# A decoder trunk on one core: the low halves of split weights made by another engine, a mean shift moved off TensorE, and 52 weight blocks multiplied in wider instructions

## The chip, the core and the metric

The kernel runs on one core of one Trainium2 chip. The core has a matrix engine (TensorE; PE in the profile, PEld for its weight loads), three engines for elementwise work (VectorE = DVE, ScalarE = ACT, GpSimd = POOL), an engine that mostly issues DMAs (SyncE = SP), and 16 DMA engines. Each engine works through its own queue in order; queues wait for each other by semaphores. The metric is the device time of one execution in microseconds, lower is better; the median of several runs is quoted.

## What is computed

Two decoder layers on one sequence of 256 tokens, model width 2048, everything in float32. Layer 0 mixes by causal pooling, layer 1 by dilated attention; each is followed by a gated feed-forward network with a short causal convolution, and each of the four sub-blocks ends in `h = layer_norm(alpha * h + sub_block(h))` with alpha = 4^(1/4). Cut to what matters here:

```python
def layer_norm(x, g, b):
    mu = jnp.mean(xf, axis=-1, keepdims=True)
    var = jnp.mean(jnp.square(xf - mu), axis=-1, keepdims=True)
    y = (xf - mu) * lax.rsqrt(var + LN_EPS) * g + b
...
def pool_mixer(h, w_in, w_grp, scale, w_out):
    p = h @ w_in                       # 2048 x 2048, four groups of 512 channels
    pooled = trailing means over 2, 4, 8, 16 tokens, minus p
    mixed = per group pooled @ w_grp, * scale
    return mixed @ w_out
...
def conv_ffn(h, w_up, conv_w, conv_b, w_down):
    c = causal width-3 convolution of (h @ w_up) + conv_b
    gate, val = jnp.split(c, 2, axis=-1)
    return (jax.nn.silu(gate) * val) @ w_down      # hidden width 5504
...
for i in range(2):
    mix = pool_mixer(h, ...) if i == 0 else dilated_attention(h, k_shared, v_shared, ...)
    h = layer_norm(ALPHA * h + mix, ln1_g[i], ln1_b[i])
    h = layer_norm(ALPHA * h + conv_ffn(h, ...), ln2_g[i], ln2_b[i])
```

The weights are some 380 MB and are read from HBM once.

## The kernel before

**Precision.** A float32 product is made from float32r products by splitting both factors into a high part (the value rounded to float32r) and a low part (the value minus its high part): high x high, high x low and low x high are summed, low x low is dropped. An activation tile is stored as `[128, 4, 2, 258]`: four blocks of 128 channels, high and low part, 256 tokens and two more columns.

**Units.** The weights are cut into 364 units of mostly 512 x 512 (four row blocks of 128, four column blocks of 128, 1 MB); a few have three row or column blocks. `group` (L153) and `group_tm` (L162) append units; four units in a row (or three or two, in the down-projections) sum up into the same four PSUM banks, and the last of them calls `post`, which empties the banks. `run_units` (L102) does the units in order. For unit i it first calls `ahead(i)` (L87), then issues unit i's matmuls, then the functions that earlier units put off with `later(n, fn)`, then `post`. All of it is written out by hand in program order; each engine's queue has that order.

**Loads and splits.** `do_load` (L60) brings unit i + 5 from HBM by SyncE's queue into one of three raw tiles, so a load waits until the split of the unit three before has let go of its tile. `do_split` (L70) runs three units ahead of TensorE and makes `wh` (high) and `wl` (low), with four tiles each. There are two ways. Two units in three: ScalarE rounds raw to `wh` (L82), VectorE computes `wl = raw - wh` (L83). Every third unit from unit 6 on: ScalarE writes `wl = -raw` rounded (L77), then `wh` (L78), and a DMA issued by GpSimd adds raw to `wl` in memory (L79). Either way the raw tile is free when `wl` is done.

**Matmuls.** `mm_quad` (L126) does a unit with the weights stationary. For each row block k and column block m, mode "ab" issues two matmuls: `wh` on high and low part of the activations side by side (512 columns, L141), and `wl` on the high part (256 columns, L142); high and low products land in the two halves of a bank, and `post` has to add the halves. Modes "a" and "x" issue three matmuls of 256 (258) columns into the same half: L144, L145, L146. In the last unit of a group the column blocks are done one after another, so that their banks can be emptied one after another. `group_tm` uses the activations as the stationary side, with 512 columns of weights (L170 to L172).

**Which units have which mode.** The up-projections from the third pair of groups on, the down-projections of layer 0 apart from the last, and the attention's projections for K and Q from the second group on are "ab". The pooling's input projection (`add_in`, L462), its group products, the second pair of up-projection groups of each layer, and everything that goes through `add_last` (L398) are "a": the pooling's output projection (16 units), the attention's output projection (16) and the last part of layer 0's down-projection (12 units, four of them of three row blocks). The first groups behind a LayerNorm are "x".

**Residual and LayerNorm.** `resid_last(c)` (L242) adds bank m to block m of `H[c]` (L247, L249), the quarter c of the stream, while TensorE is still at the next block. To keep sums of squares small, a per-token shift, found from the first quarter (`shift`, L289: a matmul with ones, L291, a unit after quarter 0), is taken off the whole stream. For quarter 0 VectorE subtracts it (L299). For the others: where the sub-block is the first to be added to H (both mixers), the subtraction is part of the scaling by alpha in `pre` (L311); in the last down-projection of layer 0 it is instead a thirteenth product for each bank, a matmul of one row, minus ones times the shift (L148, with `neg1` from L216). Then follow sums and sums of squares (`fold`, L270), the scaled copies `XP` that the "x" units use (`xp`, L316), and the statistics (`chain`, L326) with normalisation of H by VectorE (`norm`) and the affine step and the split of the activations (`affine`, `lo`) in the units after.

**Pooling.** `pool_post` (L406) copies the banks out by ScalarE (L412) and builds window sums on VectorE (L416 to L423).

Of the kernel before, what the change touches and what calls it, by code (L numbers as in the profile page):

```python
# [10 lines left out]
F32R = mybir.dt.float32r  # L11
I32 = mybir.dt.int32
AF = mybir.ActivationFunctionType
OP = mybir.AluOpType
# [3 lines left out]
T = 256  # L18
P = 128
# [3 lines left out]
ALPHA = 4.0 ** 0.25  # L23
# [9 lines left out]
def trunk(ctx: ExitStack, tc: tile.TileContext, x, pool_w_in, pool_w_grp, pool_scale, pool_w_out,  # L33
          attn_w_q, attn_w_o, shared_w_k, shared_w_v, ffn_w_up, ffn_conv_w, ffn_conv_b, ffn_w_down,
          ln1_g, ln1_b, ln2_g, ln2_b, out):
    nc = tc.nc
    V, A, PE = nc.vector, nc.scalar, nc.tensor
    ctx.enter_context(tc.manual_schedule())

    const = ctx.enter_context(tc.tile_pool(name="const", bufs=1))  # L40
# [13 lines left out]
    raw, wh, wl = {}, {}, {}  # L54
# [15 lines left out]
    def do_split(i):  # L70
        r = raw.pop(i)
        shape = [P, r.shape[1], r.shape[2]]
        wh[i] = wp.tile(shape, F32R, name=f"wh{i}", tag="wh")
        wl[i] = wp.tile(shape, F32R, name=f"wl{i}", tag="wl")
        if i >= 4 and i % 3 == 0:

            A.activation(wl[i], r, AF.Copy, scale=-1.0)  # L77
            A.copy(wh[i], r)  # L78
            nc.gpsimd.dma_start(wl[i], r, accum_op=OP.add)  # L79
            return  # L80
        for j, s in enumerate(pieces(i, r.shape[1])):
            A.copy(wh[i][:, s], r[:, s])  # L82
            V.tensor_tensor(wl[i][:, s], r[:, s], wh[i][:, s].bitcast(F32), OP.subtract)  # L83
            if i == 0 and j == 0:
                x_quad(0, (1,))
# [37 lines left out]

    XW = T + 2

    def mm_quad(xq, ps, first, last, mode, mid, shifted):  # L126
        def go(h, l):
            nk, nb = h.shape[1], h.shape[2] // P
            order = [(k, m) for k in range(nk) for m in range(nb)]
            if last:  # L130
                order = [(k, m) for m in range(nb) for k in range(nk)]
            if first:
                for m in range(nb):
                    ps.append(bank("acc"))
            q = xq()
            n = XW if mode == "x" else T
            for i, (k, m) in enumerate(order):
                c = slice(m * P, (m + 1) * P)
                st, sp = first and k == 0, last and k == nk - 1
                if mode == "ab":  # L140
                    PE.matmul(ps[m], h[:, k, c], q[:, k, :, :T], start=st, stop=False)  # L141
                    PE.matmul(ps[m][:, :T], l[:, k, c], q[:, k, 0, :T], start=False, stop=sp)  # L142
                else:
                    PE.matmul(ps[m][:, :n], h[:, k, c], q[:, k, 0, :n], start=st, stop=False)  # L144
                    PE.matmul(ps[m][:, :n], h[:, k, c], q[:, k, 1, :n], start=False, stop=False)  # L145
                    PE.matmul(ps[m][:, :n], l[:, k, c], q[:, k, 0, :n], start=False, stop=sp and not shifted)  # L146
                    if sp and shifted:
                        PE.matmul(ps[m][:, :n], neg1[0:1, :], ST["cs"][0:1, :], start=False, stop=True)  # L148
                if mid is not None and i == 7:
                    mid()  # L150
        return go

    def group(w, r0s, c0, ncol, xqs, post, mode="ab", mids=(), shifted=False):  # L153
        ps = []
        for j, (r0, nr) in enumerate(r0s):
            last = j == len(r0s) - 1
            units.append((w[r0:r0 + nr, c0:c0 + ncol],
                          mm_quad(xqs[j], ps, j == 0, last, mode, mids[j] if j < len(mids) else None, shifted),
                          (lambda: post(ps)) if last else None))


# [46 lines left out]
    rows4 = [(512 * j, 512) for j in range(4)]  # L208

    pools = {}  # L210
    H, XC, XP, ST = {}, {}, {}, {}
# [1 line left out]
    ident = const.tile([P, P], F32, name="ident")  # L213
    ones = const.tile([P, 1], F32, name="ones")
    one1 = const.tile([P, P], F32, name="one1")
    neg1 = const.tile([1, P], F32R, name="neg1")  # L216
    ones4 = const.tile([P, P], F32R, name="ones4")
    epst = const.tile([P, 1], F32, name="epst")
    inv = const.tile([P, 1, 16], F32, name="inv")
# [3 lines left out]
    xsrcs = [lambda j=j: XC[j] for j in range(4)]  # L223
# [18 lines left out]
    def resid_last(c, first, lay, which, after):  # L242
        def post(ps):
            for m in range(4):
                y = H[c][:, m, :]
                if first and c == 0:
                    V.scalar_tensor_tensor(y, y, ALPHA, ps[m][:, :T], op0=OP.mult, op1=OP.add)  # L247
                else:
                    V.tensor_tensor(y, y, ps[m][:, :T], OP.add)  # L249
                if c == 3 and m % 2 == 1:  # L250
                    square(3, m - 1)
            if c == 0:
                s = fold(H[0], None, "S0", F32R)
                later(1, lambda: shift(s, first, lay, which))
            elif c < 3:
                n = 3 if c == 1 and not first else 1
                later(n, lambda: stats(c))
                later(n + 1, lambda: xp(c, lay, which))
            else:
                folds(3)  # L260
                xp(3, lay, which)
                later(2, lambda: chain(ps[0], lay, which, after))
        return post
# [25 lines left out]
    def shift(s, first, lay, which):  # L289
        ps = bank("shift")  # L290
        PE.matmul(ps[:, :T], ones4, s, start=True, stop=True)  # L291
        cs = lnp.tile([P, T], F32R, name="cs", tag="cs")
        A.copy(cs, ps[:, :T])
        ST["cs"] = cs
        cb = cs.bitcast(F32).unsqueeze(1).to_broadcast([P, 4, T])
        ST["S"] = ST["Q"] = None

        def one():
            V.tensor_tensor(H[0], H[0], cb, OP.subtract)  # L299
            if first:  # L300
                pre(1)
            stats(0)

        def two():
            xp(0, lay, which)
            if first:
                pre(2)
                pre(3)

        def pre(q):  # L310
            V.scalar_tensor_tensor(H[q], H[q], ALPHA, cb, op0=OP.mult, op1=OP.subtract)  # L311

        later(1, one)
        later(2, two)
# [82 lines left out]

    def add_last(w, rows, srcs, first, lay, which, after=None):  # L398
        for c in range(4):
            group(w, rows, 512 * c, 512, srcs, resid_last(c, first, lay, which, after), mode="a", shifted=c > 0 and not first)  # L400


    PADW = 16
    pooled_q, mixed_q = {}, {}

    def pool_post(g):  # L406
        def post(ps):
            pp = pools["pool"]
            w = 2 << g
            p = pools["pb"][g % 2]  # L410
            for m in range(4):
                A.copy(p[:, m, PADW:], ps[m][:, :T])  # L412
            cur, lo, sh = p, 0, 1
            while sh < w:
                nxt = pp.tile([P, 4, PADW + T], F32, name="sw", tag="sw", bufs=2)
# [3 lines left out]
            n = w - 1  # L419
# [4 lines left out]
                                   op0=OP.mult, op1=OP.subtract)  # L424
# [35 lines left out]
            before.setdefault(min(q + 1, 3), []).append(lambda s=s, pv2=pv2: A.copy(H[q][:, s, :], pv2))  # L460

    def add_in(g, mids=()):  # L462
        group(pool_w_in[0], rows4, 512 * g, 512, xsrcs, pool_post(g), mode="a", mids=mids)

    def add_grp(g):
        group(pool_w_grp[0, g], [(0, 512)], 0, 512, [lambda: pooled_q[g]], grp_post(g), mode="a")
# [189 lines left out]
    scale = 1.0 / math.sqrt(P)  # L656
# [98 lines left out]
    with tc.tile_pool(name="start", bufs=1) as stp:  # L755
# [18 lines left out]
                for i in range(WARM):  # L774
                    PE.matmul(warm[:, :P], one1, one1, start=True, stop=True)
        V.memset(ones, 1.0 / D)
        A.activation(neg1, one1[0:1, :], AF.Copy, scale=-1.0)
        A.activation(ones4, one1, AF.Copy, scale=4.0 / D)
        V.memset(epst, EPS)
        for c in range(16):  # L780
# [108 lines left out]
```

## Time and profile before

| | |
|---|---|
| median of 3 runs | 2100.22 us |
| lowest and highest | 2100.1, 2101.11 us |
| span of the profiled execution, first to last instruction | 2098.8 us |
| HBM read, per span | 380 MB, 182 GB/s |
| DMA engines: share of the loads' queue / of GpSimd's queue | 52.7% / 29.0% |

The profile gives the span of the execution, 2098.8 us, and no other time for it; the device time of the runs contains a little more than from the first to the last instruction. Times are us unless marked ns. A row of groups shows line, engine, operation, output and inputs, shape, count, then busy time and mean duration in ns, then the engine's idle time before these instructions and what ended it. A matmul's own duration is its passage through a pipeline; what a matmul costs in a stream is the distance from its start to the next start. In rows by window the counts of instructions in brackets include those that began before the window; the last three numbers are the granted TensorE clock (1.00 is full speed), the mean busy share of the DMA engines, and GB/s.

### The profile page before, as it was taken

What the parts mean: (1) busy time and instruction counts of PE and PEld (TensorE: products, weight loads), DVE (VectorE), ACT (ScalarE), POOL (GpSimd) and SP (SyncE); (2) the same over time, 40 slices, a digit from 0 to 9 for tenths busy, and PEclk for the clock granted to TensorE, in tenths of its full rate; (3) what the DMA queues carried; (4) which work ended last, traced back from release to release, by engine and by line L of the source; (5) the groups of instructions that cost most, each with busy time, mean ns of one, the idle gap of its engine ahead of it and who ended that gap; (6) DMA issues with size and microseconds to landing.
All of it is one profiled execution on the core that took longest, in us unless ns stands there. A gap on an engine that the chain in (4) does not pass through costs nothing.

```text
span 2098.8 us, 30899 instructions
## 1 busy us (share of the span) xinstructions
PE 2075.0 (99%) x12959; PEld 1863.9 (89%) x12959; DVE 1137.6 (54%) x1586; ACT 1235.0 (59%) x1266; POOL 112.9 (5%) x158
## 2 busy tenths in 40 slices
PE   8999999999999999999999999999999999999997
PEld 8999998888888888899888889999888888888885
DVE  5546575645644655556734555565535553554555
ACT  6555776556645646657755555586646654655663
POOL 2000000000000000000000000000000000000000
PEclk9999999999999999999999999999999999999999
DMA  8888778988888888787887778878888879888885
GB/s 249 272 242 254 221 216 270 276 250 247 240 248 260 250 235 260 221 263 202 232 243 233 221 226 234 238 205 247 241 263 259 260 231 265 246 241 253 233 243 183
DMA packets 212588, 507.59 MB, mean 242 GB/s; under 512 B 8943, under 2 KB 17797, under 8 KB 197985
## 3 DMA queue, kind: packets, MB, share of 16 engines
q1 hardware_dynamic: 194240, 381.71, 52.7%
q0 software_dynamic: 18208, 123.92, 29.0%
q8 instruction: 101, 1.65, 0.3%
q14 instruction: 39, 0.31, 0.0%
HBM read 380.01 MB, written 2.10 MB: 182 GB/s over the span
## 4 chain that ended last, share of the span: by engine, by line
PE 90%; DMA 6%; ACT 1%; issue 1%; DVE 1%; SPq 0%; POOL 0%; DVEq 0%; POOLq 0%; ACTq 0%
PE acc L141 34%; PE acc L142 17%; PE acc L144 8%; PE acc L146 8%; PE acc L145 8%; PE t L170 4%; PE t L171 4%; PE t L172 4%; DMA wl<-raw 4%; DMA raw<-in_ffn_w_down_dram 1%; DMA crow<-in_ffn_conv_w_dram 1%; DMA raw<-in_ffn_w_up_dram 0%; PE s L699 0%; PE o L739 0%; DMA xin<-in_x_dram 0%
## 5 line engine op out<-in xcount | busy, mean ns | idle before, releaser
L141 PE MATMUL acc<-xc,wh 128*128 128x512 f32 x2624 | 924.1, 396 | 0.0
L83 DVE TENSOR_TENSOR wl<-raw,wh 128x2048 fp32r<-128x2048 f32 (+2 forms) x256 | 551.9, 2160 | 522.8 <-ACT wh L82 514.3
L142 PE MATMUL acc<-xc,wl 128*128 128x256 f32 x2624 | 736.2, 281 | 0.0
L82 ACT CAST wh<-raw 128x2048 fp32r<-128x2048 f32 (+2 forms) x256 | 460.1, 1803 | 270.3 <-PE acc L141 128.7
L141 PEld LDWEIGHTS acc<-xc,wh 128*128 128x128 f32 x2624 | 495.0, 189 | 116.6
L142 PEld LDWEIGHTS acc<-xc,wl 128*128 128x128 f32 x2624 | 494.8, 189 | 0.2
L77 ACT ACTIVATE wl<-raw 128x2048 fp32r<-128x2048 f32 (+1 forms) x120 | 226.2, 1885 | 266.4 <-PE acc L142 109.1
L78 ACT CAST wh<-raw 128x2048 fp32r<-128x2048 f32 (+1 forms) x120 | 223.0, 1858 | 0.0
L79 POOL DMA_DIRECT2D wl<-raw x120 | 101.5, 846 | 1933.6 <-ACT wl L77 1484.1
L141 PE MATMUL acc<-g,wh 128*128 128x512 f32 x512 | 179.9, 396 | 0.0
L524 DVE SCALAR_TENSOR_TENSOR c<-u,cv,c 128x256 f32<-128x256 f32 x344 | 144.8, 481 | 41.3 <-ACT c L520 40.4
L146 PE MATMUL acc<-xc,wl 128*128 128x256 f32 x512 | 145.8, 285 | 6.9 <-DMA wl<-raw 6.6
L144 PE MATMUL acc<-xc,wh 128*128 128x256 f32 x512 | 145.4, 284 | 0.9 <-ACT wh L82 0.9
L145 PE MATMUL acc<-xc,wh 128*128 128x256 f32 x512 | 145.0, 283 | 0.0
L142 PE MATMUL acc<-g,wl 128*128 128x256 f32 x512 | 143.6, 280 | 0.0
L171 PE MATMUL t<-wl,g 128*128 128x512 f32 x344 | 135.6, 394 | 1.9 <-DMA wl<-raw 1.9
L170 PE MATMUL t<-wh,g 128*128 128x512 f32 x344 | 136.1, 396 | 0.0
L172 PE MATMUL t<-wh,g 128*128 128x512 f32 x344 | 135.4, 394 | 0.0
L141 PEld LDWEIGHTS acc<-g,wh 128*128 128x128 f32 x512 | 96.6, 189 | 22.8
L145 PE MATMUL acc<-xp,wh 128*128 128x258 f32 x384 | 109.2, 284 | 0.0
L144 PE MATMUL acc<-xp,wh 128*128 128x258 f32 x384 | 109.1, 284 | 0.0
L146 PE MATMUL acc<-xp,wl 128*128 128x258 f32 x384 | 107.9, 281 | 0.0
(195 smaller groups left out, 3055.4 us busy)
## 6 DMA issues: line engine op xcount, KB each, us to landing
raw<-in_ffn_w_up_dram SPq DMA_DIRECT2D x160, 1024.0 KB, 5.6
wl<-raw POOLq DMA_DIRECT2D x111, 1024.0 KB, 7.7
raw<-in_ffn_w_down_dram SPq DMA_DIRECT2D x80, 1024.0 KB, 6.7
raw<-in_pool_w_out_dram SPq DMA_DIRECT2D x16, 1024.0 KB, 6.4
raw<-in_shared_w_k_dram SPq DMA_DIRECT2D x16, 1024.0 KB, 5.3
raw<-in_attn_w_q_dram SPq DMA_DIRECT2D x16, 1024.0 KB, 5.8
raw<-in_shared_w_v_dram SPq DMA_DIRECT2D x16, 1024.0 KB, 5.9
raw<-in_attn_w_o_dram SPq DMA_DIRECT2D x16, 1024.0 KB, 6.0
```

The costliest lines, as they stand in the source:

```text
L77: A.activation(wl[i], r, AF.Copy, scale=-1.0)
L78: A.copy(wh[i], r)
L82: A.copy(wh[i][:, s], r[:, s])
L83: V.tensor_tensor(wl[i][:, s], r[:, s], wh[i][:, s].bitcast(F32), OP.subtract)
L141: PE.matmul(ps[m], h[:, k, c], q[:, k, :, :T], start=st, stop=False)
L142: PE.matmul(ps[m][:, :T], l[:, k, c], q[:, k, 0, :T], start=False, stop=sp)
L144: PE.matmul(ps[m][:, :n], h[:, k, c], q[:, k, 0, :n], start=st, stop=False)
L145: PE.matmul(ps[m][:, :n], h[:, k, c], q[:, k, 1, :n], start=False, stop=False)
L146: PE.matmul(ps[m][:, :n], l[:, k, c], q[:, k, 0, :n], start=False, stop=sp and not shifted)
L170: PE.matmul(ps[t], xh, h[:, k, :], start=j == 0 and k == 0, stop=False)
L171: PE.matmul(ps[t], xh, l[:, k, :], start=False, stop=False)
L172: PE.matmul(ps[t], xl, h[:, k, :], start=False, stop=j == len(r0s) - 1 and k == nk - 1)
```

## The change

Three edits.

1. Every unit is split the first way: `wh` by ScalarE, `wl` by VectorE. The branch with the negated copy and the adding DMA goes.
2. The one-row products go, with `neg1` and the parameter `shifted`. In the last down-projection of layer 0, `pre` now subtracts the shift from quarters 1 to 3 of H on VectorE; `pre(1)` is called in `one`, `pre(2)` and `pre(3)` in `two`, as it is for the mixers.
3. All of `add_last` (44 units) and the pooling's input projection for groups 0 and 1 (8 units) become mode "ab". `resid_last` adds the second half of each bank by a second VectorE addition, `pool_post` likewise for those two groups.

```diff
@@ do_split
-        if i >= 4 and i % 3 == 0:
-
-            A.activation(wl[i], r, AF.Copy, scale=-1.0)
-            A.copy(wh[i], r)
-            nc.gpsimd.dma_start(wl[i], r, accum_op=OP.add)
-            return
         for j, s in enumerate(pieces(i, r.shape[1])):
             A.copy(wh[i][:, s], r[:, s])
             V.tensor_tensor(wl[i][:, s], r[:, s], wh[i][:, s].bitcast(F32), OP.subtract)
@@ mm_quad
-                    PE.matmul(ps[m][:, :n], l[:, k, c], q[:, k, 0, :n], start=False, stop=sp and not shifted)
-                    if sp and shifted:
-                        PE.matmul(ps[m][:, :n], neg1[0:1, :], ST["cs"][0:1, :], start=False, stop=True)
+                    PE.matmul(ps[m][:, :n], l[:, k, c], q[:, k, 0, :n], start=False, stop=sp)
@@ resid_last
                 else:
                     V.tensor_tensor(y, y, ps[m][:, :T], OP.add)
+                V.tensor_tensor(y, y, ps[m][:, T:], OP.add)
@@ shift
         def one():
             V.tensor_tensor(H[0], H[0], cb, OP.subtract)
-            if first:
-                pre(1)
+            pre(1)
             stats(0)
 
         def two():
             xp(0, lay, which)
+            pre(2)
+            pre(3)
+
+        def pre(q):
             if first:
-                pre(2)
-                pre(3)
-
-        def pre(q):
-            V.scalar_tensor_tensor(H[q], H[q], ALPHA, cb, op0=OP.mult, op1=OP.subtract)
+                V.scalar_tensor_tensor(H[q], H[q], ALPHA, cb, op0=OP.mult, op1=OP.subtract)
+            else:
+                V.tensor_tensor(H[q], H[q], cb, OP.subtract)
@@ add_last
-            group(w, rows, 512 * c, 512, srcs, resid_last(c, first, lay, which, after), mode="a", shifted=c > 0 and not first)
+            group(w, rows, 512 * c, 512, srcs, resid_last(c, first, lay, which, after))
@@ pool_post
                 A.copy(p[:, m, PADW:], ps[m][:, :T])
+                if g < 2:
+                    V.tensor_tensor(p[:, m, PADW:], p[:, m, PADW:], ps[m][:, T:], OP.add)
@@ add_in
-        group(pool_w_in[0], rows4, 512 * g, 512, xsrcs, pool_post(g), mode="a", mids=mids)
+        group(pool_w_in[0], rows4, 512 * g, 512, xsrcs, pool_post(g), mode="ab" if g < 2 else "a", mids=mids)
@@ start
-        A.activation(neg1, one1[0:1, :], AF.Copy, scale=-1.0)
```

(The default mode of `group` is "ab".)

More of the change, by code (lines that the diff above doesn't have):

```diff
@@ L124, in trunk, with mm_quad @@
     XW = T + 2
-    def mm_quad(xq, ps, first, last, mode, mid, shifted):
+    def mm_quad(xq, ps, first, last, mode, mid):
         def go(h, l):
@@ L151, in mm_quad, with group @@
         return go
-    def group(w, r0s, c0, ncol, xqs, post, mode="ab", mids=(), shifted=False):
+    def group(w, r0s, c0, ncol, xqs, post, mode="ab", mids=()):
         ps = []
@@ L157, in group @@
             units.append((w[r0:r0 + nr, c0:c0 + ncol],
-                          mm_quad(xqs[j], ps, j == 0, last, mode, mids[j] if j < len(mids) else None, shifted),
+                          mm_quad(xqs[j], ps, j == 0, last, mode, mids[j] if j < len(mids) else None),
                           (lambda: post(ps)) if last else None))
@@ L215, in trunk @@
     one1 = const.tile([P, P], F32, name="one1")
-    neg1 = const.tile([1, P], F32R, name="neg1")
     ones4 = const.tile([P, P], F32R, name="ones4")
@@ L293, in shift @@
         A.copy(cs, ps[:, :T])
-        ST["cs"] = cs
         cb = cs.bitcast(F32).unsqueeze(1).to_broadcast([P, 4, T])
```

## The prediction

> **What bounds the kernel now.** First the page: what is busy, and what the chain that ended last consists of.
>
> ```profile
> span 2098.8 us, 30899 instructions
> PE 2075.0 (99%) x12959; PEld 1863.9 (89%) x12959; DVE 1137.6 (54%) x1586; ACT 1235.0 (59%) x1266; POOL 112.9 (5%) x158
> PE 90%; DMA 6%; ACT 1%; issue 1%; DVE 1%; SPq 0%; POOL 0%; DVEq 0%; POOLq 0%; ACTq 0%
> ```
>
> TensorE is busy for 99% of the span, and nine tenths of the chain that ended last are matmuls. So only two kinds of thing can shorten this kernel: fewer or cheaper steps of TensorE, and fewer waits of TensorE. VectorE and ScalarE have room on average. Next the table of waits, for TensorE and its weight loads alone (total us, how often, longest).
>
> ```profile
> PEld acc L146 <- DMA wl<-raw: 8.3, 5, 5.2
> PE acc L146 <- DMA wl<-raw: 7.1, 3, 5.0
> PEld t L171 <- DMA wl<-raw: 2.3, 1, 2.3
> PE t L171 <- DMA wl<-raw: 1.9, 1, 1.9
> ```
>
> Every wait that matters is for one thing: a low part `wl` that an adding DMA had still to deliver. There are six (five at L146, one at L171), 10.6 us in the weight-load rows. A low part made by VectorE was waited for once:
>
> ```profile
> PE acc L146 <- DVE wl L83: 0.2, 1, 0.2
> ```
>
> The longest wait comes early, in unit 6. The timeline of TensorE and two windows around it (the clock is the entry after the engines):
>
> ```profile
> 46.36 0.28 PE L145 MATMUL acc<-xc,wh 128*128 128x256 f32 x1
> 51.66 0.58 PE L146 MATMUL acc<-xc,wl 128*128 128x256 f32 x1 [5.02 <-DMA wl<-raw]
> 52.04 0.41 PE L144 MATMUL acc<-xc,wh 128*128 128x256 f32 x1
> 52.25 0.41 PE L145 MATMUL acc<-xc,wh 128*128 128x256 f32 x1
> ```
> ```profile
> 46.00:59.00 13.00, 7.98 (x51) 7.78 (x50) 5.92 (x5) 6.01 (x9) 0.00 (x0) 0.74 0.74 224
> 50.00:55.00 5.00, 3.34 (x15) 3.34 (x16) 1.42 (x1) 1.90 (x1) 0.00 (x0) 0.50 0.45 136
> ```
>
> After the wait the steps are 0.21 us apart (52.04 to 52.25), and the granted clock is 0.50 in that window: the stall is paid for a second time, at half clock.
>
> **The change, part by part.** *Low parts by VectorE.* The adding DMAs go, and with them the six waits. The early one: 13.0 us passed for some 49 steps (51 records, of which two began before the window). At 0.119 us a step, derived below, they need 5.8, so this stall costs about 7.1 with its half clock. The other five: 10.6 less 5.2 leaves 5.4; a weight load starts its wait a little ahead of its matmul (5.2 against 5.0 above), so I take 0.1 off each, and put 0.1 back for the slower restart behind it. Together 7.1 + 5.4 = **12.5 us**, if VectorE is in time everywhere. What it takes on, from the groups by shape:
>
> ```profile
> L83 DVE TENSOR_TENSOR wl<-raw,wh 128x2048 fp32r<-128x2048 f32 x225 | 515.4, 2292 | 496.8 <-ACT wh L82 496.1
> L77 ACT ACTIVATE wl<-raw 128x2048 fp32r<-128x2048 f32 x111 | 212.8, 1917 | 242.6 <-PE acc L142 102.0 <-DMA raw<-in_ffn_w_down_dram 47.8 <-PE acc L146 25.1
> L249 DVE TENSOR_TENSOR h<-h,acc 128x256 f32<-128x256 f32 x40 | 15.0, 417 | 14.2 <-PE acc L146 13.2 <-PE acc L148 1.0
> L311 DVE SCALAR_TENSOR_TENSOR h<-h,cs 128x1024 f32<-128x1024 f32 x6 | 7.1, 1220 | 0.0
> ```
>
> 111 whole units at 2.292 us are 254 us, and nine units of three blocks at three quarters of that are 16: VectorE goes from 1138 us to about 1408. ScalarE loses L77: 213 us, and nine small ones at three quarters, some 13; it falls from 1235 to about 1009. Each unit takes TensorE 5.6 to 5.7 us and VectorE 2.3 for its low part, so on average this hides. It must also hide where VectorE is fullest. Those are the stages behind a LayerNorm, where normalising, the convolution and the low parts of the activations share its queue. There a new subtraction delays all that stands behind it in order: the low part of the next unit, and the activations' low parts. The fullest one, in layer 1, by window, then by the rows of VectorE and of the matmul that needs the result:
>
> ```profile
> 1380.00:1410.00 30.00, 30.00 (x253) 30.00 (x252) 23.70 (x31) 28.09 (x36) 1.69 (x2) 1.00 0.68 202
> ```
> ```profile
> 1398.97 1.23 DVE L538 TENSOR_TENSOR c<-u,c 128x1024 f32<-128x1024 f32 x1 [1.55 <-ACT u L537]
> 1400.77 2.29 DVE L83 TENSOR_TENSOR wl<-raw,wh 128x2048 fp32r<-128x2048 f32 x1 [0.57 <-ACT wh L82]
> 1406.24 0.28 PE L146 MATMUL acc<-xc,wl 128*128 128x256 f32 x1
> ```
>
> Two moved units fall into these 30 us: VectorE would have 28.3 of 30, ScalarE 24.3. Bound there is ScalarE today, VectorE afterwards. The walk: the low part of unit 241 ends at 1403.06 and is needed at 1406.24, 3.2 us of slack, the least of any unit behind the first few. In front of it goes the subtraction of unit 240, +2.29; away go VectorE's two waits for ScalarE, 1.55 and 0.57, since ScalarE is 1.9 us earlier by the L77 that it no longer does. Net +0.2: slack stays at about 3.0. I therefore cost this part at nothing, with that slack as the cover; without it, each microsecond of VectorE beyond 3 is a microsecond of TensorE.
>
> The early unit 6 needs its own walk: its raw tile and VectorE before it.
>
> ```profile
> 37.64 1.92 ACT L77 ACTIVATE wl<-raw 128x2048 fp32r<-128x2048 f32 x1 [2.36 <-DMA raw<-in_pool_w_in_dram]
> 40.98 1.16 DVE L423 SCALAR_TENSOR_TENSOR po<-sw,pb 128x964 f32<-128x964 f32 x1
> ```
>
> The raw tile is there at 37.6, so `wh` (now first in ScalarE's queue) is done at 39.6. VectorE is busy with the pooling until 42.1, then subtracts until 44.4. The low part is needed at 46.5, one step after 46.36: 2.1 us to spare.
>
> Loads: a raw slot comes free when its split is done, and the SyncE queue waits for that.
>
> ```profile
> SPq L68 <- DMA wl<-raw: 1342.2, 119, 16.3
> wl<-raw POOLq DMA_DIRECT2D x111, 1024.0 KB, 7.7
> ```
>
> Today a moved unit holds its raw tile for two ScalarE passes and a DMA of 7.7 us (median), 11.5 us in all. Afterwards it is 1.9 + 2.3 = 4.2 us and the time in VectorE's queue. So loads start earlier, the DMA engines lose the second pass over those tiles, and I expect no new wait for a load.
>
> *Shift products.* Twelve one-row matmuls at L148 go. What one costs, from the starts around it:
>
> ```profile
> 921.48 0.28 PE L145 MATMUL acc<-g,wh 128*128 128x256 f32 x1
> 921.61 0.28 PE L146 MATMUL acc<-g,wl 128*128 128x256 f32 x1
> 921.82 0.38 PE L148 MATMUL acc<-cs,neg 1*128 1x256 f32 x1
> 922.12 0.39 PE L144 MATMUL acc<-g,wh 128*128 128x256 f32 x1
> 922.35 0.28 PE L145 MATMUL acc<-g,wh 128*128 128x256 f32 x1
> ```
>
> From 921.61 to 922.35 pass 0.74 us for three steps; the two that stay need 0.24. One shift product thus costs 0.50 us, far more than a step, because its neighbours are spread too; twelve are **6.0 us**. In their place VectorE gets three subtractions of a quarter of H, by L311's 1.22 us each 3.7 us, in the last down-projection of layer 0, where the additions follow at their own pace; nothing on TensorE waits for them within two units. Hidden.
>
> *52 units as 512 plus 256 columns.* The same columns in two instructions, not three. Whole stretches of both forms, from one start to another:
>
> ```profile
> 168.34 0.28 PE L144 MATMUL acc<-mixed,wh 128*128 128x256 f32 x1
> 225.43 0.28 PE L144 MATMUL acc<-xp,wh 128*128 128x258 f32 x1
> 431.55 0.39 PE L141 MATMUL acc<-xc,wh 128*128 128x512 f32 x1
> 566.48 0.40 PE L141 MATMUL acc<-g,wh 128*128 128x512 f32 x1
> ```
>
> Between the first two lie ten units of 48 steps: 57.09 us, 5.709 a unit, 0.119 a step. Between the others lie 24 units of 32 steps: 134.93 us, 5.622 a unit. The difference is 0.087 us a unit. 48 whole units and four of three blocks count as 51: **4.4 us**. By the ends of such rows it could be nothing (if the gain came from the stage) or about 6. The Trainium skill, in "TensorE: Matmul & The Clock Gate", section "Back-to-back issue gap", gives for an isolated warm matmul N/2.4 + 2.5 ns; by that one instruction less is worth 2.5 ns, some 2 us over 816 triples. The trace's 5.4 ns per triple (0.087 us over 16) is twice that, and I stay with the trace. VectorE pays for it with 4 more additions of 0.417 us per group: twelve groups of residual additions and two of pooling, 23 us, each behind the end of a group. For all but the last block they run while TensorE does the next block (its steps last 1.4 us a block there), so a chain gets about 0.4 us longer. The nearest thing waiting is the column-sum product, a unit later.
>
> **The sum.** 12.5 + 6.0 + 4.4 = 22.9 us off the span of 2098.8: 2075.9. The runs' median of 2100.22 lies 1.4 above that span (launch and end are not in it, and nothing there changes), so 2100.2 - 22.9 = **2077.3 us**.
>
> **The rivals.**
> *VectorE late behind the LayerNorms.* Three LayerNorms are followed by such a stage, and the start is a fourth tight place; the covers are 3.0 and 2.1 us by walks that assume everything else in place. If VectorE is 2 us too late for each of the four, 8 us come back: 2085. For it: 28.3 us of 30. Against: just ahead of that stage VectorE still idles for 5.2 us, so it enters it without a backlog:
>
> ```profile
> 1372.45 1.23 DVE L353 TENSOR_TENSOR h<-h,rm 128x1024 f32<-128x1024 f32 x1 [5.22 <-ACT rm L349]
> ```
>
> *The columns bring nothing.* If 0.087 us belongs to the stage (other tiles, other DMA traffic), 4.4 goes: 2081.7. Against: two long stretches hardly vary.
> *A low part is late all the time.* One mechanism could make the kernel slower. VectorE works in order, and a subtraction now stands in every unit behind the previous group's evacuation and ahead of the next one's. Where it waits for `wh` (496 us of such waits in L83's row), all behind it waits too; the raw slot is released late, the next load starts late, and TensorE pauses in each round. It decides from 22.9 / 120 = 0.19 us per moved unit; at 0.3 us it is 36 us, 2113. For it: those waits. Against: today two thirds of the units live this way, with one wait of 0.2 us.
> *Waits replaced by load waits early on.* If the early stall stays, half to all of its 7.1 us come back, 2081 to 2084.
>
> **How the numbers follow.** The forecast holds with 0.70 (its own range 2074 to 2080: 1.5 us for the columns term, 1 for the stalls, 1 for runs). VectorE late: 0.13. Columns nothing: 0.06. Early stall kept: 0.04. Slower all the time: 0.04. In between, near no change: 0.03. The predicted time is 2077.3, the likeliest case. The range goes from 2073 (columns at 6 us, and some of the run's spread) to 2086, which takes in the late VectorE and the early stall. Faster by over 0.2% (4 us, about what a measurement here can tell from no change) has 0.93, same 0.03, slower 0.04.
>
> **What would show it.** TensorE's table of waits has no `wl` of a DMA, and no entry over 1 us for `wl` of L83. Windows from 46 to 59 us show clock 1.00 and about 110 steps. No one-row matmul; the starts around 921 us are 0.12 apart or follow the 0.23/0.12 pattern. The 48 units of whole size take 5.62 us each. VectorE about 1435 us busy, ScalarE 1009, and the software DMA queue almost empty. The prediction is wrong if TensorE waits for VectorE behind a LayerNorm by more than 3 us, if the unit time of the new pairs stays at 5.70, or if a load of unit 7 or 8 takes the place of the early stall.

## The result, and the profile after

The changed kernel takes 2079.14 us (median of 4 runs, 2078.62 to 2079.52); the kernel before, beside it, 2100.16 us (2099.67 to 2101.11). The ratio is 0.9895, with a 95% interval from 0.9881 to 0.9909. So it is 21.0 us, or 1.05%, faster. Forecast were 2077.3 us and 22.9 us.

The page of the changed kernel, the lines that answer to those shown of before: the span, the busy times, the chain by engine, and GpSimd's software queue (packets, MB, share of 16 engines).

```profile
span 2077.2 us, 28936 instructions
PE 2062.0 (99%) x12131; PEld 1819.3 (88%) x12131; DVE 1417.2 (68%) x1765; ACT 1029.2 (50%) x1145; POOL 11.4 (1%) x38
q0 software_dynamic: 928, 0.44, 0.1%
PE 98%; DVE 1%; DMA 0%; SPq 0%; issue 0%; ACT 0%; DVEq 0%
```

TensorE now makes up 98% of the chain that ended last, where it made up 90%; the DMA's 6% are gone. VectorE has taken on 280 us and ScalarE has lost 206. That VectorE rose from 54% to 68% cost nearly nothing, which is only understood by looking at what TensorE still waits for. The whole table of waits of its matmuls (total us, how often, longest):

```profile
PE xT L449 <- DMA xin<-in_x_dram: 2.2, 2, 1.8
PE warm L769 <- DVE epst L772: 1.1, 1, 1.1
PE acc L340 <- ACT dg L334: 0.3, 1, 0.3
```

No wait for a low part is left. The first two rows belong to the first microseconds, before any weight is multiplied. The third is new: one product of the LayerNorm's scale, at L340, waits 0.3 us for the copies `dg` that ScalarE makes of the LayerNorm's statistics. It is the only wait of a matmul inside the kernel, and further down it turns out to come from the fuller VectorE. (The table of the weight loads adds one wait of 0.2 us, for VectorE in the attention.)

Next, windows of the changed kernel (time, then busy time and count of PE, PEld, DVE, ACT and POOL, then the granted clock, the DMA share and GB/s): around the old stall of unit 6, and the stretch of layer 1 that the prediction took as the fullest (17 us earlier now).

```profile
46.00:59.00 13.00, 13.00 (x111) 12.80 (x111) 10.59 (x8) 9.85 (x15) 0.00 (x0) 1.00 0.88 308
1363.00:1393.00 30.00, 30.00 (x253) 30.00 (x252) 26.92 (x30) 24.58 (x34) 0.00 (x0) 1.00 0.42 143
```

The 13 us hold 111 matmuls where they held 51, at full clock. In the second window VectorE works 26.9 of 30 us, and TensorE is not interrupted.

Both executions can be compared unit by unit, from the start of a unit's first matmul to the start of the next unit's. The span fell by 21.6 us:

| place | us |
|---|---|
| unit 6 (13.52 to 6.30) | 7.2 |
| the other waits for adding DMAs (units 48, 156, 240 to 247, 363) | 5.3 |
| shift products, units 157 to 167 | 6.0 |
| 512 plus 256 columns (pooling, pooling's output projection, last down-projection of layer 0, projection of o) | 4.4 |
| units 168 to 175, slower | -0.7 |
| the start (first weight matmul at 7.93, not 6.35; unit 0 1.0 shorter) | -0.6 |

The long stretches that the change doesn't touch, units 52 to 155 and 252 to 351, take the same time to within 0.01 us in both.

### The profile page after: what moved, and what is told of

Same layout as the page of the kernel before. It is cut to its first block, busy times and chain, and to the rows that moved or that the text cites. A ratio compares the mean times of both kernels' runs of the same rounds, so it can differ in the third digit from the quotient of the medians.

```text
span 2077.2 us, 28936 instructions
## 1 busy us (share of the span) xinstructions
PE 2062.0 (99%) x12131; PEld 1819.3 (88%) x12131; DVE 1417.2 (68%) x1765; ACT 1029.2 (50%) x1145; POOL 11.4 (1%) x38
## 4 chain that ended last, share of the span: by engine, by line
PE 98%; DVE 1%; DMA 0%; SPq 0%; issue 0%; ACT 0%; DVEq 0%
PE acc L135 44%; PE acc L136 23%; PE t L162 5%; PE t L164 5%; PE t L163 5%; PE acc L139 5%; PE acc L138 5%; PE acc L140 5%; DVE wl L77 0%; PE s L693 0%; PE o L733 0%; DVE ht L633 0%; PE pT L720 0%; DMA xin<-in_x_dram 0%; PE o L734 0%; PE s L692 0%
## 5 line engine op out<-in xcount | busy, mean ns | idle before, releaser
L77 DVE TENSOR_TENSOR wl<-raw,wh 128x2048 fp32r<-128x2048 f32 (+2 forms) x376 | 821.1, 2187 | 514.8 <-ACT wh L76 504.9
L76 ACT CAST wh<-raw 128x2048 fp32r<-128x2048 f32 (+2 forms) x376 | 685.3, 1828 | 594.3 <-PE acc L135 367.9
L135 PE MATMUL acc<-xc,wh 128*128 128x512 f32 x2752 | 969.1, 396 | 0.0
L135 PE MATMUL acc<-g,wh 128*128 128x512 f32 x688 | 241.9, 396 | 0.0
L136 PE MATMUL acc<-g,wl 128*128 128x256 f32 x688 | 193.0, 280 | 0.0
L135 PEld LDWEIGHTS acc<-g,wh 128*128 128x128 f32 x688 | 129.9, 189 | 30.6
L136 PEld LDWEIGHTS acc<-g,wl 128*128 128x128 f32 x688 | 130.0, 189 | 0.0
L138 PE MATMUL acc<-xc,wh 128*128 128x256 f32 x384 | 109.2, 284 | 0.0
L139 PE MATMUL acc<-xc,wh 128*128 128x256 f32 x384 | 108.7, 283 | 0.0
L505 ACT COPY ut<-acc 128x256 f32<-128x256 f32 x140 | 51.6, 371 | 96.3 <-PE acc L136 96.1
L135 PE MATMUL acc<-o,wh 128*128 128x512 f32 x256 | 90.4, 396 | 0.0
```

Source lines behind the costliest of these rows:

```text
L505: A.copy(t, ps[m][:, T:])
```

## The experiments

Eleven runs, of nine new kernels, were made in three sessions, each beside the kernel before: it took 2101.64 us in the first (2099.71 to 2106.26), 2102.56 in the second and 2100.92 in the third. The first five change one thing in the kernel before.

**Low parts by VectorE, alone.** The branch goes; shift products and columns stay.

```diff
-        if i >= 4 and i % 3 == 0:
...
-            nc.gpsimd.dma_start(wl[i], r, accum_op=OP.add)
-            return
```

> The kernel before with the first edit alone: all low parts by VectorE. Theory (three separate terms that add up): the six waits of TensorE for an adding DMA go and nothing else changes, 12.5 us less, about 2087.7; unit 6 takes 5.7 to 6.3 us where it took 13.5; the one-row products still cost 0.50 us each; units of three matmuls per block still take 5.70 us. Rival (the DMA traffic is what slows everything): the steps of TensorE get shorter too and nearly the whole gain of 21 us appears here, about 2079 to 2081. Second rival (the wait behind the second LayerNorm of layer 0 comes from the longer residual additions, not from the moved subtraction): no wait of TensorE for the copies dg here; by the theory there is one of some 0.4 us, since the subtraction of a moved unit stands ahead of the statistics in VectorE's queue.

Measured: 2088.13 us (2087.82 to 2088.63), ratio 0.9932, 0.9920 to 0.9944; the span is 12.6 us below before's 2098.8. Unit 6 takes 6.30 us, and its window is like the changed kernel's:

```profile
46.00:59.00 13.00, 13.00 (x111) 12.80 (x110) 10.64 (x9) 9.70 (x17) 0.00 (x0) 1.00 0.91 318
```

The long stretches between the waits keep their time to the hundredth of a microsecond although the DMA moves less, so the gain is that of the waits, not of DMA traffic. And this kernel has no wait for `dg`, where the theory expected one of 0.4 us: units 168 to 171 take 24.96 us as before. The moved subtractions alone don't cause the changed kernel's loss there; whether the longer residual additions do, as the second rival has it, is seen further down.

**Shift products as VectorE subtractions, alone.**

```diff
-            if first:
-                pre(1)
+            pre(1)
...
-            ... mode="a", shifted=c > 0 and not first)
+            ... mode="a")
```

> The kernel before with the second edit alone: the twelve one-row products replaced by three VectorE subtractions. Theory: 6.0 us less, about 2094.2, all of it inside the last down-projection of layer 0 (units 156 to 167). Rival (a one-row product only fills time that the next wait takes anyway): under 2 us less, about 2098 to 2100.

Measured: 2095.22 us (2094.72 to 2098.01), ratio 0.9969, 0.9956 to 0.9981. Units 157 to 167 show the edit without the waits elsewhere. The first matmul of unit 157 and of unit 168, in the kernel before and then in this one (start, duration):

```profile
899.11 0.28 PE L144 MATMUL acc<-g,wh 128*128 128x256 f32 x1
962.32 0.39 PE L144 MATMUL acc<-xp,wh 128*128 128x258 f32 x1
```
```profile
899.97 0.28 PE L144 MATMUL acc<-g,wh 128*128 128x256 f32 x1
957.18 0.28 PE L144 MATMUL acc<-xp,wh 128*128 128x258 f32 x1
```

63.21 us became 57.21: twelve products cost 6.00 us, 0.50 each, and VectorE's subtractions in their place cost TensorE nothing.

**The same shift product over 128 rows.** Is it the product or its one row that costs 0.50 us? Here it stays, over 128 equal rows with weights of -1/128.

```diff
-    PE.matmul(ps[m][:, :n], neg1[0:1, :], ST["cs"][0:1, :], start=False, stop=True)
+    PE.matmul(ps[m][:, :n], neg1, ST["cs"], start=False, stop=True)
...
-        A.activation(neg1, one1[0:1, :], AF.Copy, scale=-1.0)
+        A.activation(neg1, one1, AF.Copy, scale=-1.0 / P)
```

> The kernel before with the twelve shift products kept on TensorE, but over all 128 rows (weights of minus 1/128 on 128 equal rows of the shift) in place of one row. Theory A (the one-row form itself is dear: the array changes its shape, and neither the weights of it nor of its neighbours load ahead): a product becomes an ordinary step of 0.12 us, 12 x 0.38 = 4.6 us less than before, about 2095.6. Theory B (a product at the end of a bank's sum is dear whatever its rows): no change, about 2100.2.

Measured: 2096.84 us (2093.19 to 2100.02), ratio 0.9976, 0.9967 to 0.9985. One of the products with its neighbours, and the first matmul of unit 168 (that of unit 157 starts at 900.24):

```profile
922.70 0.29 PE L146 MATMUL acc<-g,wl 128*128 128x256 f32 x1
922.83 0.28 PE L148 MATMUL acc<-cs,neg 128*128 128x256 f32 x1
922.95 0.28 PE L144 MATMUL acc<-g,wh 128*128 128x256 f32 x1
...
958.84 0.29 PE L144 MATMUL acc<-xp,wh 128*128 128x258 f32 x1
```

The starts are 0.12 us apart as everywhere, and units 157 to 167 take 58.60 us, 4.61 less than before: 0.38 us of each product's 0.50 was due to its one row, the rest is that of any step. The weight loads show where the time went; first those around the one-row product in the kernel before, then that of the product over 128 rows here:

```profile
921.49 0.19 PEld L146 LDWEIGHTS acc<-g,wl 128*128 128x128 f32 x1
921.81 0.18 PEld L148 LDWEIGHTS acc<-cs,neg 1*128 1x128 f32 x1
922.12 0.19 PEld L144 LDWEIGHTS acc<-g,wh 128*128 128x128 f32 x1
```
```profile
922.71 0.19 PEld L148 LDWEIGHTS acc<-cs,neg 128*128 128x128 f32 x1
```

Over 128 rows a load starts 0.12 us ahead of its matmul (922.71 and 922.83; in the kernel before 921.49 and 921.61). The loads of the one-row product and of the product behind it start with their matmuls (921.81 and 921.82, 922.12 and 922.12): neither was made ahead, as theory A said.

**The columns, alone.** 52 units as 512 plus 256 columns; adding DMAs and shift products stay.

```diff
-            group(..., resid_last(...), mode="a", shifted=c > 0 and not first)
+            group(..., resid_last(...), shifted=c > 0 and not first)
...
-        group(pool_w_in[0], ..., mode="a", mids=mids)
+        group(pool_w_in[0], ..., mode="ab" if g < 2 else "a", mids=mids)
```

> The kernel before with the third edit alone: 52 units as 512 plus 256 columns, the adding DMAs and the one-row products kept. Theory: 0.087 us per whole unit, 4.4 us less, about 2095.8. Rival by the skill's spacing formula: 2.5 ns per triple of matmuls, 0.040 us per unit, 2.0 us less, about 2098.1. Second rival (the difference belonged to the stage): nothing, 2100.

Measured: 2096.14 us (2094.19 to 2098.41), ratio 0.9971, 0.9961 to 0.9982. The whole time also holds waits for adding DMAs, which differ between executions; the 16 units of the projection of o, 216 to 231, hold none. Their first matmul and the first one behind them, before and here:

```profile
1257.04 0.28 PE L144 MATMUL acc<-o,wh 128*128 128x256 f32 x1
1352.31 0.29 PE L144 MATMUL acc<-xp,wh 128*128 128x258 f32 x1
```
```profile
1255.20 0.40 PE L141 MATMUL acc<-o,wh 128*128 128x512 f32 x1
1349.14 0.28 PE L146 MATMUL acc<-xp,wh 128*128 128x258 f32 x1
```

95.27 us became 93.94, in the same stage with the same tiles: 1.33 for 256 triples, 5.2 ns each. "The columns bring nothing" falls. The sum over all 52 units is about 4.4 us (in units 22 to 35 1.30, in 157 to 167 0.96, in 9 to 21 0.73). The Trainium skill ("TensorE: Matmul & The Clock Gate", section "Back-to-back issue gap") would by its formula for an isolated matmul give 2.5 ns for a triple, an estimate of 2.0 us in all; the measured 5.2 ns decide against it here.

**The first moved unit alone.** Only unit 6 gets its low part from VectorE.

```diff
-        if i >= 4 and i % 3 == 0:
+        if i >= 9 and i % 3 == 0:
```

> The kernel before with one low part moved to VectorE, that of unit 6 (the adding DMAs begin with unit 9). Theory (the early stall with its half clock is one event of unit 6): 7.2 us less than before, span about 2091.6, unit 6 in 6.3 us. Rival (the next adding DMA, of unit 9, is then late in its place): under 3 us less, a wait for a DMA's low part before 75 us.

Measured: 2095.81 us (2094.11 to 2097.31), ratio 0.9974, 0.9963 to 0.9984. Unit 6 takes 6.30 us, 7.2 less, and the half clock behind it is gone:

```profile
46.00:59.00 13.00, 13.00 (x111) 12.80 (x111) 7.75 (x7) 11.37 (x16) 0.92 (x1) 1.00 0.92 275
```

The median fell by 5.1 us only, the span by 3.6. The trace says where the rest is: against the first profile of the kernel before, unit 0 took 0.9 us longer in this execution, and the units that wait for the adding DMAs that stay took longer, by 2.0 us in unit 243, 0.6 in unit 363 and 0.3 in unit 156. The landing varies: unit 243 took 7.5 us in that first profile, 9.9, 7.4 and 6.8 in the three above that keep it, and 9.5 here. Not all of that is waiting. TensorE waited there for 1.6, 2.4, 1.4, 0.8 and 2.0 us, and in the two long cases half clock followed for 3.4 us, some 1.7 us more.

**Where the new wait comes from.** The remaining kernels start from the changed one. First the rows that explain its wait for `dg`: VectorE, and then ScalarE and TensorE, at units 168 to 171 (start, duration; in brackets the idle time before and what ended it).

```profile
948.69 2.28 DVE L77 TENSOR_TENSOR wl<-raw,wh 128x2048 fp32r<-128x2048 f32 x1
950.89 0.41 DVE L240 TENSOR_TENSOR h<-h,acc 128x256 f32<-128x256 f32 x1
...
953.69 0.42 DVE L241 TENSOR_TENSOR h<-h,acc 128x256 f32<-128x256 f32 x1
...
958.78 4.48 DVE L77 TENSOR_TENSOR wl<-raw,wh 128x2048 fp32r<-128x2048 f32 x2
963.19 0.15 DVE L325 TENSOR_TENSOR sm<-sm 128x2 f32<-128x2 f32 x1
```
```profile
963.37 0.29 ACT L326 ACTIVATE sm<-sm,epst 128x2 f32<-128x2 f32 x1 [1.70 <-DVE sm L325]
963.90 1.28 ACT L334 ACTIVATE dg<-ident,sm 128x128 f32<-128x128 f32 x4 [0.23 <-DVE sm L327]
```
```profile
963.78 0.28 PE L140 MATMUL acc<-xp,wl 128*128 128x258 f32 x1
964.35 0.38 PE L340 MATMUL acc<-dg,one 128*128 128x128 f32 x1 [0.29 <-ACT dg L334]
```

The statistics of the LayerNorm (L325) are a chain of instructions of 0.15 us on two engines. They stand in VectorE's queue behind two subtractions of 2.28 us. ScalarE waits 1.70 us for them, and TensorE reaches the product first. VectorE comes to them late: a subtraction (948.69) stands ahead of the eight residual additions, four more than before, and the sums follow only then. With the subtractions alone it came there with time to spare, having idled 2.85 us, as this row of that kernel shows (its L327 is L325 here):

```profile
967.06 0.16 DVE L327 TENSOR_TENSOR sm<-sm 128x2 f32<-128x2 f32 x1 [2.85 <-ACT sm L326]
```

With the columns alone units 168 to 171 take 24.94 us, with the shift edit alone 24.85, in the changed kernel 25.61: it takes more than one of the edits. Why, the seven units 163 to 169 show, in the window from the start of unit 163 to that of unit 170 (VectorE is the third entry behind the time), with the subtractions alone and then in the changed kernel:

```profile
924.35:966.45 42.10, 42.10 (x330) 40.02 (x329) 32.05 (x47) 21.30 (x28) 0.00 (x0) 1.00 0.53 180
920.39:958.03 37.64, 37.64 (x251) 34.42 (x249) 36.85 (x62) 19.15 (x27) 0.00 (x0) 1.00 0.51 168
```

VectorE is busy for 76% of this stretch with the subtractions alone (82% with the shift edit alone, 76% with the columns alone, 65% before) and for 98% in the changed kernel: the edits add to its work, and two of them shorten the time in which it has to be done. Whether two of the three would be enough was not run.

**The statistics first.** Behind each LayerNorm one split is put off by a unit, so one subtraction comes behind the statistics.

```diff
         n = max(0, min(i - 1, SP_AHEAD) if i > 2 else 0)
+        if i in [m + 1 for m in marks[:3]]:
+            n -= 1
```

> The kernel after, with the split that VectorE did just ahead of the LayerNorm statistics (one unit per LayerNorm, three in all) put off by one unit, so that the statistics stand before it in VectorE's queue. Theory (the wait of TensorE for the copies dg in the kernel after is the moved subtraction standing ahead of the small statistics in order): that wait goes, units 168 to 175 take 48.0 us where they took 48.7, 0.6 us less in the span, and nothing else moves. Rival (the statistics are late because the residual additions end late): the wait stays at about 0.4 us, span unchanged.

Measured: 2077.76 us (2077.49 to 2077.98), ratio 0.9882, 0.9867 to 0.9897. VectorE's rows:

```profile
957.66 2.28 DVE L77 TENSOR_TENSOR wl<-raw,wh 128x2048 fp32r<-128x2048 f32 x1
959.86 0.15 DVE L327 TENSOR_TENSOR sm<-sm 128x2 f32<-128x2 f32 x1
...
963.68 4.49 DVE L77 TENSOR_TENSOR wl<-raw,wh 128x2048 fp32r<-128x2048 f32 x2 [2.95 <-ACT wh L76]
```

One subtraction stands ahead of the statistics instead of two. The wait for `dg` is gone, and units 168 to 171 take 24.85 us, 0.76 less. The residual additions are the same here, so on their own they don't make the wait.

**More columns.** The second groups of each layer's up-projection (16 units of three 256-column steps) also as 512 plus 256.

```diff
-            mode = "x" if x0 else "a" if q == 1 else "ab"
+            mode = "x" if x0 else "ab"
```

> The kernel after, with the second pair of up-projection groups of both layers (16 units, right behind a LayerNorm, where VectorE is fullest) also as 512 plus 256 columns; each group adds four copies of ScalarE and four additions of VectorE. Theory (a cover of some 3 us is left there): 16 x 0.09 = 1.4 us less, about 2077.7. Rival (VectorE has become the bound behind the LayerNorms): TensorE waits for low parts of L77 in units 44 to 60 and 240 to 256, and the time rises by 2 us or more, 2081 or above.

Measured: 2077.09 us (2076.40 to 2077.37), ratio 0.9879, 0.9864 to 0.9893. The four groups of four units gain 0.33, 0.34, 0.32 and 0.36 us, 1.35 together, 0.084 a unit. The wait for `dg` stays, as it should.

**Both, and the rest of the pooling.** The two edits above, and all input projections of the pooling as 512 plus 256.

```diff
-                if g < 2:
-                    V.tensor_tensor(p[:, m, PADW:], p[:, m, PADW:], ps[m][:, T:], OP.add)
+                V.tensor_tensor(p[:, m, PADW:], p[:, m, PADW:], ps[m][:, T:], OP.add)
...
-        group(pool_w_in[0], ..., mode="ab" if g < 2 else "a", mids=mids)
+        group(pool_w_in[0], ..., mode="ab", mids=mids)
```

> Both edits before together, and the pooling's input projection for its other two groups (8 units, at the start) as 512 plus 256 columns too. If all terms add: 0.6 + 1.4 + 0.7 = 2.7 us less than the kernel after, about 2076.4. If the start is too tight (cover of 2.1 us by the walk, and 1.7 us of additions go in front of the low part of unit 6): a wait of TensorE for L77 before 55 us, and no gain from the pooling's part.

Measured: 2075.64 us (2075.04 to 2078.42), ratio 0.9875, 0.9860 to 0.9889. Units 1 to 7 give another 0.5 us, where 0.7 was expected for all eight; unit 0, whose length differs from execution to execution, can't be compared.

To see whether that is more than chance, the changed kernel and this one ran once more, side by side.

> The kernel after once more, on the same chip as the next two. Theory (the 0.6 us by which it started later in its first profile, and the half clock there, belong to that execution's loads of x and not to the change): first weight matmul before 7.2 us and a span of 2075.5 to 2077.2; the wait for dg behind the second LayerNorm of layer 0 again 0.3 to 0.5 us. Rival (the change delays the start): first weight matmul at 7.9 us again.

> The kernel with the statistics first and all 24 further units in wide instructions, beside the kernel after: 2.4 to 3.0 us below it. If the smaller runs before were a matter of the chip's day: under 1 us below it.

Measured: 2078.56 us (2078.39 to 2079.05; ratio 0.9892, 0.9877 to 0.9908) and 2075.88 us (2075.59 to 2076.53; ratio 0.9880, 0.9866 to 0.9893). The better one is 2.7 us below the changed kernel, and their runs don't overlap. The changed kernel's second profile has the wait for `dg` again, but its first weight matmul starts at 7.10 us, not at 7.93: the late start belonged to the first execution.

**How much more VectorE could carry.** Every third unit's subtraction is issued twice, which repeats work and leaves the output as it is.

```diff
             V.tensor_tensor(wl[i][:, s], r[:, s], wh[i][:, s].bitcast(F32), OP.subtract)
+            if i >= 4 and i % 3 == 0:
+                V.tensor_tensor(wl[i][:, s], r[:, s], wh[i][:, s].bitcast(F32), OP.subtract)
```

> The kernel after, with the low part of every third unit computed twice by VectorE (the second pass writes the same values), so that the suspected cost, the moved subtractions, is there once more: VectorE gains 270 us, to 1690, 81% of the span. Theory (covers of about 3 us behind the LayerNorms, one extra subtraction of 2.3 us in front of each tight unit): small waits there, 0 to 4 us more in all, 2079 to 2083; nothing in the long stretches between. Rival (VectorE's order makes TensorE wait in every round): over 20 us more, about 2100 or above, with waits for L77 in all stretches.

Measured: 2097.41 us (2095.51 to 2097.79), ratio 0.9973, 0.9964 to 0.9983. The span is 2095.3, 18.1 us above the changed kernel's, with VectorE at 1677 us, 80%. I had expected 0 to 4 us, so that was wrong; the rival, a loss in every stretch, was wrong too. TensorE's largest waits, and a long stretch against one behind the LayerNorm:

```profile
PE acc L323 <- DVE S L271: 2.8, 1, 2.8
PE acc L142 <- DVE u L489: 2.4, 1, 2.4
PE acc L140 <- ACT wh L76: 1.6, 1, 1.6
PE acc L142 <- DVE wl L79: 1.4, 1, 1.4
PE acc L324 <- DVE Q L271: 1.1, 1, 1.1
```
```profile
300.00:560.00 260.00, 260.00 (x1519) 228.61 (x1518) 218.03 (x253) 129.58 (x131) 0.55 (x2) 1.00 0.56 195
965.00:990.00 25.00, 23.74 (x171) 23.66 (x172) 21.45 (x21) 14.96 (x25) 0.00 (x0) 0.86 0.38 129
```

In 260 us VectorE is busy for 218, 84%, and TensorE never stops; units 52 to 119 and 252 to 351 take what they take in the changed kernel. The loss sits at the joints: 7.0 us in units 168 to 171 (granted clock 0.86 in the window there), 4.3 in units 240 to 247, 1.9 in 176 to 183, 1.7 in 44 to 47, 1.4 in 157 to 167, and most of the rest at the start.

## Why the prediction was right, and where it was off

**Six waits, 12.5 us: right.** The two profiles give 12.5 (7.2 and 5.3), the kernel with that edit alone 12.6. Unit 6 is 7.2 against 7.1: the second half of this price, the half clock behind the stall, was real, since the unit moved alone brings it too. (13.0 less 5.8 is 7.2; the prediction has 7.1.) The walks held. Unit 6's low part, and that of unit 241, with the first matmul that needs each:

```profile
42.61 2.28 DVE L77 TENSOR_TENSOR wl<-raw,wh 128x2048 fp32r<-128x2048 f32 x1
47.11 0.28 PE L140 MATMUL acc<-xc,wl 128*128 128x256 f32 x1
1383.31 2.28 DVE L77 TENSOR_TENSOR wl<-raw,wh 128x2048 fp32r<-128x2048 f32 x1
1388.97 0.28 PE L140 MATMUL acc<-xc,wl 128*128 128x256 f32 x1
```

They are ready 2.2 and 3.4 us ahead; 2.1 and 3.0 were forecast. Behind unit 6 no low part of the changed kernel is ready less than 3.1 us ahead (unit 45).

**Shift products, 6.0 us: right,** 6.00 in the kernel with that edit alone. The loads show why the neighbours are spread: neither the one-row product's weights nor those of the product behind it were loaded ahead, and over 128 rows the same product costs an ordinary step.

**Columns, 4.4 us: right in sum.** The ten units 26 to 35 of the changed kernel, from the first start to the one behind them:

```profile
160.65 0.40 PE L135 MATMUL acc<-mixed,wh 128*128 128x512 f32 x1
216.79 0.28 PE L138 MATMUL acc<-xp,wh 128*128 128x258 f32 x1
```

56.14 us, 5.614 a unit, where 5.62 was forecast and 5.709 was before.

**The step that failed: VectorE's new work at nothing.** The prediction took the column-sum product, a unit later, as the nearest thing that waits for the residual additions, and looked at the low parts for the cover. It did not walk the statistics behind the LayerNorm, which stand in the same queue behind the subtractions. Nor was the stretch that it took as the fullest the one that counted: there VectorE came to 26.9 of 30 us and cost nothing, while in units 163 to 169, where all three edits meet, it was busy for 36.9 of 37.6. The term was 0.7 us instead of 0 (units 168 to 175), shown by putting one split off, which takes all of it away. It is the rival "VectorE late behind the LayerNorms" in small: it came at one place of its four, 0.7 us instead of 2, and for the statistics instead of a low part. The doubled subtractions show that rival's place to be the right one to fear, and the rival "late all the time" to be wrong in its mechanism: at 84% in steady state nothing is lost.

**What else is missing of 22.9.** The span fell by 21.6: 12.5 + 6.0 + 4.4 less 0.7 less 0.6 at the start, which was that execution's. That is 1.3 of the 1.8 us by which the median lies above the forecast. The other 0.5 lie outside the span, of which the prediction says that nothing there changes. Its 1.4 us set a median of several executions against the span of a single one. Where time and span of the same execution are on record, the time is longer by 1.7 to 1.9 us in every run of the kernels with adding DMAs; by 2.0 to 2.2 us in the kernel with the first edit alone, and by 1.8 to 2.3, 2.0 in the mean, in the changed one. So some 0.3 us came with the first edit; what they are stays open. In the third session the two medians, 2100.92 and 2078.56, lie 22.4 us apart: the kernel before had medians from 2100.16 to 2102.56 us in the sessions, so the gain is not known to better than a microsecond or two.

**Busy times.** VectorE was forecast at 1435 us and measured at 1417, ScalarE at 1009 and 1029. Successive instructions overlap a little (two subtractions in a row take 4.48 us, not 4.57), which the count times the mean leaves out. The traces settle it: the durations of VectorE's instructions add up to 294 us more than before and those of ScalarE's to 224 us less, close to the 297 and 226 of the forecast, but the overlaps grew by 14 us on VectorE and shrank by 18 on ScalarE.

## What to carry to other kernels

Price a stall of TensorE with the clock behind it: 5.0 us of waiting cost 7.2. Before an engine that looks idle takes on bulk work, walk not only the consumers of that work but every short chain that stands behind it in the same queue, above all the statistics of a normalisation, where 2.3 us of bulk ahead of an instruction of 0.15 us reach TensorE once the engine has no idle time left ahead of it. Look for that place where all parts of a change meet, and not only where the engine is fullest today. And give a product with one row a second look: spread over all 128 rows it cost a quarter.

## What the runs showed of the hardware

**One row costs more than 128.** Between steps of 128 rows, a product over one row adds 0.50 us, with what it spreads its neighbours by, and one over 128 rows 0.12. The weights of the one-row product and of the next one start to load less than 0.01 us ahead of their matmuls, those of the others 0.12 us ahead.

**Two instructions for three.** 512 plus 256 columns instead of three times 256 save 0.08 to 0.09 us in a unit of 16 triples.

**An adding DMA doesn't land at a fixed time.** At 7.7 us (median) for 1 MB it had room in most units. Where it had none, it showed: for unit 243 it landed 10.8 to 12.4 us after its issue in five executions, TensorE waited 0.8 to 2.4 us, and the unit took 6.8 to 9.9 us, with half clock behind the two longest waits. The kernel before spread over 6.6 us in 17 runs of one session, the changed one, without such DMAs, over less than 1 in four; but another kernel without them spread over 3.4 in four, so they are not shown to be the whole cause.

**Half clock after an idle stretch, even a short one.** After the 5-us stall of unit 6 the clock record of the kernel before shows half clock for 6.8 us; 2.5 of these lie in the stall itself, and the other 4.4 make up the 2.2 us that unit 6 lost beyond its wait. Shorter waits can bring it as well: in the kernel with unit 6 moved alone, a wait of 1.99 us in unit 243 was followed by half clock for 3.4 us. In the kernel with doubled subtractions a wait of 2.44 us was not, so the length of the wait alone doesn't decide. In the changed kernel's first execution the start shows half clock too:

```profile
5.00:10.00 5.00, 2.83 (x13) 2.65 (x14) 2.14 (x4) 1.99 (x5) 0.00 (x0) 0.77 0.76 251
10.00:15.00 5.00, 5.00 (x40) 5.00 (x40) 3.36 (x6) 3.19 (x7) 0.00 (x0) 0.89 1.05 377
```

TensorE idles for 2.2 of the 5 us (its longest wait there is the 1.8 us for the input), and half clock follows for 3.4 us. The Trainium skill ("TensorE: Matmul & The Clock Gate", section "Part 1: The HAM clock gate") names about 3.4 us of idleness as what brings the half clock, and as the busy time that ends it. The two lengths, 3.4 and 6.8 us, are one and two of these; the 2.2 us of idleness here and the 1.99 us in unit 243 were shorter.
